# Thirteen dots at the boundaries and in the index scores, their low parts by transfer; wide block pairs in both feed-forwards

## The chip, the cores and the metric

The kernel runs on one core of a Trainium2 chip. The metric is the device time of one execution in microseconds (us). Before the change the median of three timed executions is 1220.28 us (1219.72 to 1220.76).

The core has five engines that each work through their own list of instructions in order: PE multiplies matrices (PEld is its weight load), DVE and ACT work element by element, POOL and SP here issue most of the transfers between HBM and the on-chip memory. An instruction that waits for another engine holds up all that stands behind it on its own engine.

## What is computed

Two layers of a decoder trunk on 512 positions of width 1024, all float32. Layer 0 has stick-breaking attention, layer 1 the indexer-selected sparse attention (DSA). Each mixer and each feed-forward is preceded by a norm whose shift, scale and gate come from the vector c.

```python
def conv_ffn(h, w_up, conv_w, conv_b, w_down):
    S = h.shape[1]
    u = h @ w_up
    up = jnp.pad(u, ((0, 0), (CONV_W - 1, 0), (0, 0)))
    y = conv_b
    for j in range(CONV_W):
        y = y + up[:, j:j + S] * conv_w[j]
    gate, val = jnp.split(y, 2, axis=-1)
    return (jax.nn.silu(gate) * val) @ w_down
```

The shift, scale and gate of a layer are c times a 1024 x 6144 matrix plus a bias: 48 columns of 128 numbers for each layer, six groups of eight. In the DSA layer the projection of h gives queries (16 heads of 128), one latent of 128, index queries (8 heads of 64), index keys and head weights; the index scores, a sum over the eight heads of relu(qi . ki) times a weight, choose the keys.

## The kernel before, in words

**Float32 by parts.** A weight chunk is 128 x 1024 float32 (512 KB). SP loads it into a place of the ring `raw` (`chunk_raw`), ACT copies it to the rounded high part `whi` (`split_hi`, a copy shown at L613), and then the low part `wlo` = raw - whi is made in one of two ways. `split_lo` (L622) is one DVE subtraction. `split_sum` (its ACT line is L630, its transfer L631) is two steps: ACT writes minus the *raw* chunk, rounded, into `wlo`, and POOL then issues a transfer that reads the chunk from HBM a second time and adds it into `wlo`. Inside the planned feed-forwards the same pair of steps stands at L1491 (ACT) and L1495 (POOL). `mm3` (L663 to L665) multiplies three times: high by high, then **low weight** by high, then high by low; so the low part is wanted by the second matmul of a product.

**The adaLN dots.** One of the 48 columns is one DVE instruction over a loaded 128 x 1024 chunk and c (`ada_dot`, L691). Layer 1 has 48 of them, numbered (1, group, column). Before the change they are done in feed-forward 0 (37, groups 0 to 4 but for three), in the DSA layer (three, `LATE_DOTS`) and in feed-forward 1 (eight, group 5).

**Boundaries.** `boundary` joins two stages: it ends a projection (eight row blocks m, tiles pt_l), adds them to x, and while the norm of the new x is worked out PE already runs the next projection's first four row blocks (tiles pt_first): two from the scaled but unnormed x (`xs`), two from the normed `hh`. The chunks of those four are split in the same loop: the third one's high part in step m = 6, its low part in m = 7, the fourth one's right after the loop. Boundary 0 leads to feed-forward 0, boundary 1 (which has a `begin`) to the DSA layer and its index scores, boundary 2 to feed-forward 1. Places of `raw` come free when a chunk has been split; then SP loads the next.

**Index scores.** For each of the eight index heads h PE makes three score products z (tiles of 256, 384 and 512 columns, two banks), ACT takes each one's relu (L1990), DVE adds it up; the matmuls of the next projections (pt_lat, then pt_q of the chunks dq) stand between them. After heads 0, 1, 4 and 6 a chunk dq is split with `prefetch`: low part of the chunk before, high part of the next one, low part at once.

**Feed-forwards.** 22 blocks j of 128 columns for gate and val each. Blocks 0 to 6 are plain. Blocks from 7 on are computed as pairs of 256 columns with seven products instead of eight (a1, d1, a2, e, d2, c1, c2), twelve matmuls each: four chunks of the weight, times high and low of the activation (eight matmuls of 256 columns) and low weight times high (four). For a block in `MERGED` the high and low activation stand side by side, so that the eight become four matmuls of 512 columns (L1594); the second half lands in the other half of the bank, and DVE adds it to the result after each evacuation (`side`, six additions of 128 x 256 a block). `down` multiplies the finished blocks by the down matrix, its low part by DVE, or by transfer (`DOWN_DMA`); the result is added to x by DVE (L785), or scaled by ACT (L1694) and added by a transfer (L1697, `X_DMA`). In `ACT_DMA` the low part of a block's activation is made by transfer.

`ffn_plan` orders all of it: each step is a job with an engine, a duration and what it waits for. `Plan.order` runs PE's jobs in the order written, and lets every other engine take, whenever it is free, the ready job with the earliest due time. That order is then written out as the engines' instruction lists. `LEADS`, the free times at the start and `DOT_SPAN` are the numbers it works with.

Of the kernel before, what the change touches and what calls it, by code (L numbers as in the profile page):

```python
# [21 lines left out]
KT = D // P  # L22
# [40 lines left out]
DOWNS_7 = [[(7, 1), (8, 2), (9, 2), (10, 1), (11, 2), (12, 2), (13, 1), (14, 1), (15, 1), (16, 2), (17, 1), (18, 2), (19, 2),  # L63
# [10 lines left out]
DOT_SPAN = [(10, 320), (0, 150)]  # L74
PLAIN_DMA = [[(4, 0), (4, 1), (5, 0), (5, 1), (6, 0)], [(4, 0), (4, 1), (5, 1), (6, 0), (6, 1)]]
DOWN_DMA = [[6, 13, 22], [0, 3, 4, 6, 8, 12, 13, 15, 16, 17, 20, 22]]
LEADS = [{'plain': 33.5, 'r': 20.0, 'sum': 16.0, 'down': 13.5, 'T': 40.0, 'last': 36.5, 'bias': 12.5},
         {'plain': 78.5, 'r': 3.5, 'sum': 0.5, 'down': 6.5, 'T': 8.5, 'last': 11.0, 'bias': 15.5}]
DOT_GROUPS = [[(1, 0), (1, 1), (1, 2), (1, 3), (1, 4)], [(1, 5)]]
LATE_DOTS = [(1, 4, 5), (1, 4, 6), (1, 4, 7)]  # L80
FFN_BIAS = [(1, 12), (1, 17)]
MERGED = [[], [10, 11, 12, 13, 14, 15, 16, 17, 18, 19, 20, 21]]
X_DMA = [[0, 1, 2, 3, 5, 7, 8, 10, 14, 18, 19, 21, 23], []]
ACT_DMA = [[3, 4, 18], []]
XT = 2

# [15 lines left out]
class Plan:  # L102
# [44 lines left out]
    def order(self):  # L147
# [23 lines left out]
        out = []  # L171

        def ready(j):
            if any(a.end is None for a in j.after) or any(a.start is None for a in j.behind):
                return None
            t = max((a.end + (a.lag if a.engine != j.engine or a.lag > 1 else 0.0) for a in j.after), default=0.0)
            return max([t] + [a.start for a in j.behind])

        while len(out) < len(self.jobs):
# [4 lines left out]
            while moved:  # L184
                moved = False
                for e, q in queues.items():
                    if not q or free[e] > now:
                        continue
                    can = [(r, i) for i, j in enumerate(q[:1] if e == "PE" else q) for r in [ready(j)] if r is not None and r <= now]
                    if not can:  # L190
                        continue
                    j = q.pop(min(can)[1] if e == "DMA" else can[0][1])
# [18 lines left out]
def ffn_plan(l):  # L211
# [3 lines left out]
    p = Plan(dict(DVE=13.0, ACT=12.0, SP=-5.0, DMA=-5.0, POOL=-5.0))  # L215
# [11 lines left out]
    for n, t in enumerate((-9, -9, 0.0, 1.5, 6.3, 7.5)):  # L227
# [315 lines left out]
def kernel_body(ctx, tc, xT, wst, cst, smalls, crow, ccol, relb, outT):  # L543
# [152 lines left out]

    def ada_steps(n):
# [104 lines left out]
    def boundary(n, last, O, l, gate, nxt, first, place, begin=None, after_scale=None):  # L802
# [9 lines left out]
        goals = {0: last[2], 1: last[3], 2: first[0], 4: first[1], 6: first[2]}  # L812

# [12 lines left out]
        for m in range(KT):  # L826
# [19 lines left out]
            split_lo()  # L846
# [12 lines left out]
        split_lo()  # L859
# [24 lines left out]
        for k in range(KT + 1):  # L884
# [544 lines left out]
    def ffn_layer(l, first, man):  # L1429
        with ExitStack() as st:  # L1430
# [23 lines left out]
            split_lo()  # L1454
# [304 lines left out]
    def dsa_layer(l, first, man):  # L1759
        with ExitStack() as st:  # L1760
# [118 lines left out]
            with ExitStack() as si:  # L1879
# [100 lines left out]
                for h in range(IDX_HEADS):  # L1980
# [12 lines left out]
                    if h in (0, 1, 4, 6):  # L1993
                        prefetch(pos["i"])
# [64 lines left out]
            with ExitStack() as sa:  # L2059
# [62 lines left out]
                def late_dots(n):  # L2122
                    for _ in range(n):
                        (_, g, f), raw = raw_dots.pop(0)
                        ada_dot(mod[l][:, g * KT + f:g * KT + f + 1], raw)
                        if f == KT - 1:
                            ada_sum(l, g)
# [335 lines left out]
```

## Time and profile before

| | |
|---|---|
| median of three executions | 1220.28 us |
| the profiled execution | 1219.72 us |
| its span in the trace (1.8 us lie around it) | 1217.9 us |
| granted TensorE clock | 1.00 |
| stick-breaking layer | 0 to 238 us |
| boundary 0 | 238 to 280.5 |
| feed-forward 0, plain blocks and block pairs | 280.5 to 335, 335 to 586 |
| boundary 1 | 586 to 626 |
| index scores | 634 to 659 |
| choice of keys, projections, DSA heads | to 846 |
| boundary 2 | 846 to 891 |
| feed-forward 1, of it block pairs | 891 to 1193, 946 to 1193 |
| end | to 1217.9 |

The rows of the timeline shown below read: start in us, duration in us, engine, line, operation, output <- inputs, shape, and in brackets the engine's idle time ahead of it with what ended it. SPq and POOL rows of DMA_DIRECT2D are issues of transfers, not the transfers themselves. A matmul's duration overlaps the next one's; the distance of two starts is what it costs.

### The profile page before, as it was taken

What the parts mean: (1) busy time and instruction counts of PE and PEld (TensorE: products, weight loads), DVE (VectorE), ACT (ScalarE), POOL (GpSimd) and SP (SyncE); (2) the same over time, 40 slices, a digit from 0 to 9 for tenths busy, and PEclk for the clock granted to TensorE, in tenths of its full rate; (3) what the DMA queues carried; (4) which work ended last, traced back from release to release, by engine and by line L of the source; (5) the groups of instructions that cost most, each with busy time, mean ns of one, the idle gap of its engine ahead of it and who ended that gap; (6) DMA issues with size and microseconds to landing.
All of it is one profiled execution on the core that took longest, in us unless ns stands there. A gap on an engine that the chain in (4) does not pass through costs nothing.

```text
span 1217.9 us, 18663 instructions
## 1 busy us (share of the span) xinstructions
PE 1211.9 (100%) x6768; PEld 1023.7 (84%) x6768; DVE 1040.5 (85%) x1786; ACT 785.7 (65%) x1348; POOL 218.3 (18%) x240
## 2 busy tenths in 40 slices
PE   9999999999999999999999999999999999999998
PEld 6888787788899999999888778777888998888887
DVE  5899889999989889887788996668998989889883
ACT  5587786467677667666556357774676576676650
POOL 0000000000112111111001357774001112111100
PEclk9999999999999999999999999999999999999999
DMA  9678685624999989797622311144459787777651
GB/s 376 234 194 216 194 225 196 198 73 138 245 235 247 257 233 248 211 248 191 201 70 71 103 52 53 52 124 139 136 155 216 213 186 161 181 180 174 159 132 69
DMA packets 66651, 212.77 MB, mean 175 GB/s; under 512 B 7808, under 2 KB 8576, under 8 KB 66560
## 3 DMA queue, kind: packets, MB, share of 16 engines
q1 hardware_dynamic: 50400, 166.88, 41.3%
q0 software_dynamic: 16160, 44.71, 21.0%
q8 instruction: 53, 0.87, 0.3%
q14 instruction: 38, 0.31, 0.1%
HBM read 205.25 MB, written 2.11 MB: 170 GB/s over the span
## 4 chain that ended last, share of the span: by engine, by line
PE 94%; DVE 4%; ACT 1%; issue 1%; DVEq 0%; ACTq 0%
PE pt_d L1686 16%; PE pt_a L1598 10%; PE pt_u L1567 6%; PE pt_d L1598 5%; PE pt_a L1594 4%; PE pt_u L1571 3%; PE pt_b L1598 3%; PE pt_q L663 2%; PE pt_q L665 2%; PE pt_q L664 2%; PE pt_qk L663 2%; PE pt_qk L664 2%; PE pt_qk L665 2%; PE pt_l L663 2%; PE pt_l L665 2%; PE pt_l L664 2%
## 5 line engine op out<-in xcount | busy, mean ns | idle before, releaser
L1686 PE MATMUL pt_d<-actlo,dnhi 128*128 128x512 f32 x288 | 112.7, 391 | 0.0
L1686 PE MATMUL pt_d<-acthi,dnhi 128*128 128x512 f32 x288 | 112.6, 391 | 0.0
L1495 POOL DMA_DIRECT2D wlo<-wst x40 | 34.7, 867 | 363.7 <-ACT wlo L1491 296.1
L1483 ACT ACTIVATE whi<-raw 128x1024 fp32r<-128x1024 f32 x72 | 75.7, 1053 | 27.4 <-PE pt_a L1598 17.5
L613 ACT ACTIVATE whi<-raw 128x1024 fp32r<-128x1024 f32 x80 | 84.0, 1052 | 1.2 <-PE pt_o L665 0.9
L1567 PE MATMUL pt_u<-hh,whi 128*128 128x512 f32 x320 | 75.8, 389 | 0.0
L1686 PE MATMUL pt_d<-acthi,dnlo 128*128 128x512 f32 x288 | 73.5, 390 | 0.0
L1567 PEld LDWEIGHTS pt_u<-hh,whi 128*128 128x128 f32 x320 | 60.1, 188 | 12.5
L622 DVE TENSOR_TENSOR wlo<-raw,whi 128x1024 fp32r<-128x1024 f32 x51 | 62.0, 1219 | 3.1 <-ACT whi L613 2.8
L1686 PEld LDWEIGHTS pt_d<-actlo,dnhi 128*128 128x128 f32 x288 | 54.2, 188 | 10.2
L1686 PEld LDWEIGHTS pt_d<-acthi,dnhi 128*128 128x128 f32 x288 | 54.2, 188 | 10.0
L1686 PEld LDWEIGHTS pt_d<-acthi,dnlo 128*128 128x128 f32 x288 | 53.1, 188 | 10.3
L1598 PE MATMUL pt_a<-hh,whi 128*128 128x256 f32 x432 | 60.4, 283 | 0.0
L1598 PEld LDWEIGHTS pt_a<-hh,whi 128*128 128x128 f32 x432 | 57.5, 191 | 2.3
L622 POOL TENSOR_TENSOR wlo<-raw,whi 128x1024 fp32r<-128x1024 f32 x18 | 44.0, 2452 | 84.9 <-PE pt_q L664 46.1
L691 DVE SCALAR_TENSOR_TENSOR ada<-ada,cond 128x1024 f32<-128x1024 f32 x45 | 54.8, 1218 | 3.9 <-DMA ada<-wst 3.8
L1598 PE MATMUL pt_a<-hh,wlo 128*128 128x256 f32 x360 | 57.6, 282 | 0.0
L1306 DVE TENSOR_TENSOR_SCAN mz<-mz,diag 128x128 f32<-128x128 f32 (+1 forms) x64 | 52.4, 818 | 3.4 <-ACT mz L1301 3.2
L1874 DVE CUSTOM_DVE_ANT_0 L<-z,L,cols 128x128 f32<-128x128 f32 (+3 forms) x60 | 32.5, 547 | 26.2 <-PE tr L2170 19.9
L1598 PEld LDWEIGHTS pt_a<-hh,wlo 128*128 128x128 f32 x360 | 51.8, 191 | 2.9
L691 DVE SCALAR_TENSOR_TENSOR raw<-raw,cond 128x1024 f32<-128x1024 f32 x42 | 52.6, 1279 | 1.4 <-ACT cond L1127 1.3
L1506 POOL DMA_DIRECT2D whi<-wst x30 | 25.9, 864 | 152.6 <-ACT whi L1503 60.9
(391 smaller groups left out, 3750.2 us busy)
## 6 DMA issues: line engine op xcount, KB each, us to landing
raw<-wst SPq DMA_DIRECT2D x211, 512.0 KB, 4.9
wlo<-wst POOLq DMA_DIRECT2D x51, 512.0 KB, 7.5
ada<-wst SPq DMA_DIRECT2D x49, 512.0 KB, 5.3
raw<-wst SPq DMA_DIRECT2D x48, 384.0 KB, 4.6
whi<-wst POOLq DMA_DIRECT2D x30, 256.0 KB, 5.3
dnlo<-wst POOLq DMA_DIRECT2D x15, 384.0 KB, 7.3
th<-relb SPq DMA_DIRECT2D x16, 256.0 KB, 3.3
x<-xt POOLq DMA_DIRECT2D x13, 256.0 KB, 6.8
```

Source lines behind the costliest of these rows:

```text
L613: act.activation(hi[:, :n], raw[:, :n], AF.Copy)
L622: engine.tensor_sub(lo[:, :w], raw[:, :w], hi[:, :w].bitcast(F32))
L663: pe.matmul(out, lhsT=whi, rhs=ahi, start=start, stop=False)
L664: pe.matmul(out, lhsT=wlo, rhs=ahi, start=False, stop=False)
L665: pe.matmul(out, lhsT=whi, rhs=alo, start=False, stop=stop)
L691: dve.scalar_tensor_tensor(raw, raw, 1.0, cond, op0=OP.mult, op1=OP.mult, accum_out=dst)
L1306: dve.tensor_tensor_scan(rev, rev, diag[:, S - ns:][:, ::-1], 0.0, OP.mult, OP.max)
L1483: act.activation(W[j, i][0], R[j, i], AF.Copy)
L1567: pe.matmul(pt[j, i], lhsT=W[j, i][0][:, k * P:(k + 1) * P], rhs=hs[k][n], start=k + n == 0, stop=False)
L1594: pe.matmul(pt[j, bank, "both"], lhsT=w[:, c0 + k * P:c0 + (k + 1) * P], rhs=a[2], start=new and k == 0, stop=False, skip_group_check=True)
L1598: pe.matmul(out, lhsT=w[:, c0 + k * P:c0 + (k + 1) * P], rhs=a[n], start=new and k + n == 0, stop=part == 1 and k == 3 and what in ("a2", ...
L1686: pe.matmul(pt["dn", i], lhsT=dn[i][part][:, k * P:(k + 1) * P], rhs=A[j0 + k][n], start=part + k + n == 0, stop=part == 1 and k == j1 - j ...
```

## The change

13 of layer 1's dots leave the feed-forwards (feed-forward 0 has 27 in place of 37, feed-forward 1 five in place of eight). Three are done at each boundary, with chunks loaded into `raw` (`edge_dot`), four in the index scores after heads 0, 1, 4 and 6. At the same places DVE's subtraction goes and the low part is made by `split_sum`: three chunks at each boundary, four in the index scores, and at boundaries 0 and 2 four more each, in the loop of the norm and at the start of the feed-forward: 21 in all, while one plain chunk of feed-forward 1 goes back to DVE. In the feed-forwards nine more blocks are merged (eight in feed-forward 0, one net in feed-forward 1, 54 more side additions), and transfers take over eight more additions to x and five more low parts of activations; which down chunks go by transfer is changed (three to six, and twelve to nine). The planner's start values follow. `Plan.order` is written in another way (queues by readiness in place of a search), with the same rule.

```diff
-DOWNS_7 = [[(7, 1), (8, 2), (9, 2), (10, 1), (11, 2), (12, 2), (13, 1), (14, 1), (15, 1), (16, 2), (17, 1), (18, 2), (19, 2),
+DOWNS_7 = [[(7, 1), (8, 1), (9, 2), (10, 2), (11, 2), (12, 2), (13, 1), (14, 1), (15, 2), (16, 1), (17, 1), (18, 2), (19, 2),
...
-DOT_SPAN = [(10, 320), (0, 150)]
-PLAIN_DMA = [[(4, 0), (4, 1), (5, 0), (5, 1), (6, 0)], [(4, 0), (4, 1), (5, 1), (6, 0), (6, 1)]]
-DOWN_DMA = [[6, 13, 22], [0, 3, 4, 6, 8, 12, 13, 15, 16, 17, 20, 22]]
-LEADS = [{'plain': 33.5, 'r': 20.0, 'sum': 16.0, 'down': 13.5, 'T': 40.0, 'last': 36.5, 'bias': 12.5},
-         {'plain': 78.5, 'r': 3.5, 'sum': 0.5, 'down': 6.5, 'T': 8.5, 'last': 11.0, 'bias': 15.5}]
-DOT_GROUPS = [[(1, 0), (1, 1), (1, 2), (1, 3), (1, 4)], [(1, 5)]]
-LATE_DOTS = [(1, 4, 5), (1, 4, 6), (1, 4, 7)]
-FFN_BIAS = [(1, 12), (1, 17)]
-MERGED = [[], [10, 11, 12, 13, 14, 15, 16, 17, 18, 19, 20, 21]]
-X_DMA = [[0, 1, 2, 3, 5, 7, 8, 10, 14, 18, 19, 21, 23], []]
-ACT_DMA = [[3, 4, 18], []]
+DOT_SPAN = [(10, 320), (0, 160)]
+PLAIN_DMA = [[(4, 0), (4, 1), (5, 0), (5, 1), (6, 1)], [(4, 1), (5, 1), (6, 0), (6, 1)]]
+DOWN_DMA = [[4, 6, 13, 18, 19, 21], [0, 3, 4, 7, 8, 13, 15, 16, 20]]
+LEADS = [{'plain': 35.0, 'r': 18.5, 'sum': 14.5, 'down': 12.0, 'T': 43.0, 'last': 12.5, 'bias': 23.0},
+         {'plain': 84.5, 'r': 3.5, 'sum': 0.5, 'down': 0.5, 'T': 11.5, 'last': 15.5, 'bias': 18.5}]
+FFN_BIAS = [(1, 11), (1, 13)]
+MERGED = [[10, 11, 12, 14, 16, 19, 20, 21], [7, 8, 10, 11, 12, 14, 15, 16, 17, 18, 19, 20, 21]]
+X_DMA = [[3, 4, 5, 7, 8, 10, 12, 13, 14, 19, 20, 23], [0, 2, 6, 8, 12, 16, 19, 20, 21]]
+ACT_DMA = [[2, 4, 5, 12], [2, 4, 8, 15]]
 XT = 2
+DOTS = [(1, g, f) for g in range(6) for f in range(8)]
+EDGE_DOTS = [DOTS[:3], DOTS[30:33], DOTS[40:43]]
+KEY_DOTS = DOTS[33:37]
+LATE_DOTS = DOTS[37:40]
+FFN_DOTS = [DOTS[3:30], DOTS[43:]]
...
-
-        def ready(j):
-            if any(a.end is None for a in j.after) or any(a.start is None for a in j.behind):
-                return None
+        out, wait, later, now_ready = [], {}, {e: [] for e in queues}, {e: [] for e in queues}
+        rank = {id(j): i for q in queues.values() for i, j in enumerate(q)}
+        turn = {e: 0 for e in queues}
+        needs = {id(j): [] for j in self.jobs}
+
+        def release(j):
             t = max((a.end + (a.lag if a.engine != j.engine or a.lag > 1 else 0.0) for a in j.after), default=0.0)
-            return max([t] + [a.start for a in j.behind])
+            j.ready = max([t] + [a.start for a in j.behind])
+            heapq.heappush(later[j.engine], (j.ready, rank[id(j)], j))
...
 def ffn_dots(l):
-    jobs = [g + (f,) for g in DOT_GROUPS[l] for f in range(KT)]
+    jobs = list(FFN_DOTS[l])
     if l == 0:
-        jobs = jobs[:len(jobs) - len(LATE_DOTS)]
         for n, at in FFN_BIAS:
             jobs.insert(at, ("bias", n, "row" if ("bias", n, "col") in jobs else "col"))
     return jobs
...
-    p = Plan(dict(DVE=13.0, ACT=12.0, SP=-5.0, DMA=-5.0, POOL=-5.0))
+    p = Plan(dict(DVE=10.5, ACT=12.5, SP=-5.0, DMA=-5.0, POOL=-5.0))
...
-    for n, t in enumerate((-9, -9, 0.0, 1.5, 6.3, 7.5)):
+    for n, t in enumerate((-9, -9, -5.0, -3.0, 4.7, 5.7)):
...
+    def one_dot(d, raw):
+        l, g, f = d
+        ada_dot(mod[l][:, g * KT + f:g * KT + f + 1], raw)
+        if f == KT - 1:
+            ada_sum(l, g)
...
+        edge = list(EDGE_DOTS[n])
+
+        def edge_dot():
+            d = edge.pop(0)
+            one_dot(d, chunk_raw(("ada",) + d))
...
-            split_lo()
+            if m in (3, KT - 1):
+                split_sum()
+                edge_dot()
+            else:
+                split_lo()
             if m in goals:
                 while pos["i"] <= order.index(goals[m]):
                     split_hi()
...
         split_hi()
-        split_lo()
+        split_sum()
+        edge_dot()
...
-            if k in (4, 6):
+            if k in ((4, 6) if begin else (1, 3)):
                 split_hi()
+            if k in (2, 4) and not begin:
+                split_sum()
             if k == 6:
                 rescale(0)
         if begin:
             begin(vs[0])
-        split_lo(n=1)
+            split_lo(n=1)
         rescale(1)
...
             pts, vs = first
-            split_lo()
             es = [evac_scale(0, i, vs[i]) for i in range(2)]
             split_hi()
             split_hi(ahead=0)
             ys = [evac_conv(e) for e in es]
-            split_lo()
             es = [evac_scale(1, i, pts[2 + i]) for i in range(2)]
+            split_sum()
+            split_sum()
             warm(AF.Silu)
             ys += [evac_conv(e) for e in es]
...
                     if h in (0, 1, 4, 6):
-                        prefetch(pos["i"])
+                        split_lo()
+                        split_hi()
+                        split_sum()
+                        d = KEY_DOTS[(0, 1, 4, 6).index(h)]
+                        one_dot(d, chunk_raw(("ada",) + d))
                     elif h == 2:
```

The counts over the program: PE has 504 fewer matmuls of 256 columns and 252 more of 512; DVE 20 fewer low subtractions, eight fewer additions to x, five fewer low parts of activations, 54 more side additions; ACT 20 more copies of a chunk with minus sign, eight more scaled results, five more copies of activations; POOL issues 33 more transfers, SP as many as before (352).

**ACT at the end of boundary 0's loop.** The rows run from the splitting of the third chunk (raw_2548, raw_2552 after) to the norm's logarithm `ln`. Before:

```order
L613 ACTIVATE whi_2599<-raw_2548 128x1024
L723 ACTIVATE sqt_2615<-x3_92 128x512
L836 ACTIVATE xkz70_2617<-x3_92,sm_76 128x512
L731 ACTIVATE sqhi_2622<-sqa_2469 128x512
L613 ACTIVATE whi_2636<-raw_2597 128x1024
L757 ACTIVATE ln_2664<-pt_norm_2661,ecols_80 128x512
```

After:

```order
L642 ACTIVATE whi_2603<-raw_2552 128x1024
L758 ACTIVATE sqt_2619<-x3_92 128x512
L876 ACTIVATE xkz70_2621<-x3_92,sm_76 128x512
L766 ACTIVATE sqhi_2626<-sqa_2469 128x512
L659 ACTIVATE wlo_2631<-raw_2552 128x1024
L642 ACTIVATE whi_2644<-raw_2601 128x1024
L659 ACTIVATE wlo_2646<-raw_2601 128x1024
L792 ACTIVATE ln_2676<-pt_norm_2673,ecols_80 128x512
```

Two ACT copies to a `wlo` stand new between the sum of squares (sqhi) and `ln`: the third chunk's, and behind the fourth chunk's high part (whi_2644) the fourth's. Behind each of them POOL issues its transfer. PE's order there is unchanged: the third chunk's product starts with the first normed column (hh_2430), the fourth's stands three matmuls behind. Boundaries 1 and 2 have the same four rows.

**ACT in the index scores, head 0 to head 2.** rl is the relu of a score product z. Before:

```order
L1990 ACTIVATE rl_6568<-z_6562 128x512
L613 ACTIVATE whi_6573<-raw_6439 128x1024
L1990 ACTIVATE rl_6583<-z_6577 128x256
L1990 ACTIVATE rl_6592<-z_6586 128x384
L1990 ACTIVATE rl_6601<-z_6595 128x512
L613 ACTIVATE whi_6606<-raw_6571 128x1024
L1990 ACTIVATE rl_6616<-z_6610 128x256
L1990 ACTIVATE rl_6625<-z_6619 128x384
L1990 ACTIVATE rl_6635<-z_6628 128x512
```

After:

```order
L2037 ACTIVATE rl_6400<-z_6394 128x512
L642 ACTIVATE whi_6405<-raw_6271 128x1024
L659 ACTIVATE wlo_6407<-raw_6271 128x1024
L2037 ACTIVATE rl_6419<-z_6413 128x256
L2037 ACTIVATE rl_6428<-z_6422 128x384
L2037 ACTIVATE rl_6437<-z_6431 128x512
L642 ACTIVATE whi_6442<-raw_6403 128x1024
L659 ACTIVATE wlo_6444<-raw_6403 128x1024
L2037 ACTIVATE rl_6456<-z_6450 128x256
L2037 ACTIVATE rl_6465<-z_6459 128x384
```

The negative copy of the dq chunk (wlo_6407, wlo_6444) stands behind its high part and ahead of the next head's three relus.

**PE and DVE in feed-forward 0.** Six of the seven products of block 10, the first merged one, on PE (a1, d1, a2, e, d2, c1). Before:

```order
L1598 MATMUL pt_a<-hh,whi 128x256 x8
L1598 MATMUL pt_a<-hh,wlo 128x256 x4
L1598 MATMUL pt_d<-tt,whi 128x256 x8
L1598 MATMUL pt_d<-tt,wlo 128x256 x4
L1598 MATMUL pt_b<-hh,whi 128x256 x12
L1598 MATMUL pt_a<-tt,whi 128x256 x8
L1598 MATMUL pt_a<-tt,wlo 128x256 x4
L1598 MATMUL pt_d<-tt,whi 128x256 x8
L1598 MATMUL pt_d<-tt,wlo 128x256 x4
L1598 MATMUL pt_a<-hh,whi 128x256 x8
L1598 MATMUL pt_a<-hh,wlo 128x256 x4
```

After:

```order
L1641 MATMUL pt_a<-hh,whi 128x512 x4
L1645 MATMUL pt_a<-hh,wlo 128x256 x4
L1641 MATMUL pt_d<-tt,whi 128x512 x4
L1645 MATMUL pt_d<-tt,wlo 128x256 x4
L1641 MATMUL pt_b<-hh,whi 128x512 x4
L1645 MATMUL pt_b<-hh,whi 128x256 x4
L1641 MATMUL pt_a<-tt,whi 128x512 x4
L1645 MATMUL pt_a<-tt,wlo 128x256 x4
L1641 MATMUL pt_d<-tt,whi 128x512 x4
L1645 MATMUL pt_d<-tt,wlo 128x256 x4
L1641 MATMUL pt_a<-hh,whi 128x512 x4
L1645 MATMUL pt_a<-hh,wlo 128x256 x4
```

Each product's eight matmuls of 256 columns have become four of 512. On DVE, in the next merged block, from its second evacuation:

```order
L1681 TENSOR_TENSOR vx<-vx,pt_d 128x256
L1665 TENSOR_TENSOR gate<-gate,pt_b 128x256
L1681 TENSOR_TENSOR gate<-gate,pt_b 128x256
L1700 TENSOR_TENSOR actlo<-y_3844,acthi 128x512
L1693 TENSOR_TENSOR y_3970<-y_4035,y_3970 128x512
L1681 TENSOR_TENSOR vx<-vx,pt_a 128x256
L1717 TENSOR_TENSOR dnlo<-raw,dnhi 128x768
L1675 TENSOR_TENSOR val<-vx,pt_d 128x256
```

The side additions (L1681) of vx, gate and vx again are new rows; product c1 (pt_a from tt before it is e) waits for the second of vx, for which DVE must have done the rows ahead of it.

More of the change, by code (lines that the diff above doesn't have):

```diff
@@ L170, in order @@
         times = sorted(set(free.values()))
-        out = []
-        def ready(j):
-            if any(a.end is None for a in j.after) or any(a.start is None for a in j.behind):
-                return None
-            t = max((a.end + (a.lag if a.engine != j.engine or a.lag > 1 else 0.0) for a in j.after), default=0.0)
-            return max([t] + [a.start for a in j.behind])
+        out, wait, later, now_ready = [], {}, {e: [] for e in queues}, {e: [] for e in queues}
[3 more added lines that the diff above has]
+        def release(j):
+            t = max((a.end + (a.lag if a.engine != j.engine or a.lag > 1 else 0.0) for a in j.after), default=0.0)
+            j.ready = max([t] + [a.start for a in j.behind])
+            heapq.heappush(later[j.engine], (j.ready, rank[id(j)], j))
+        for j in self.jobs:
+            j.ready = None
+            wait[id(j)] = len(j.after) + len(j.behind)
+            for a in j.after + j.behind:
+                needs[id(a)].append(j)
+        for j in self.jobs:
+            if not wait[id(j)]:
+                release(j)
         while len(out) < len(self.jobs):
@@ L186, in order @@
                 for e, q in queues.items():
-                    if not q or free[e] > now:
+                    if free[e] > now:
                         continue
[L189 to L192, printed above, removed]
+                    if e == "PE":
+                        if turn[e] >= len(q) or q[turn[e]].ready is None or q[turn[e]].ready > now:
+                            continue
+                        j = q[turn[e]]
+                        turn[e] += 1
+                    elif e == "DMA":
+                        if not later[e] or later[e][0][0] > now:
+                            continue
+                        j = heapq.heappop(later[e])[2]
+                    else:
+                        while later[e] and later[e][0][0] <= now:
+                            r, i, j = heapq.heappop(later[e])
+                            heapq.heappush(now_ready[e], (i, j))
+                        if not now_ready[e]:
+                            continue
+                        j = heapq.heappop(now_ready[e])[1]
                     j.start, j.end = now - 1e-9, now - 1e-9 + j.us
@@ L198, in order @@
                     moved = True
+                    for n in needs[id(j)]:
+                        wait[id(n)] -= 1
+                        if not wait[id(n)]:
+                            release(n)
         return [j for j in out if j.fn]
 def ffn_dots(l):
-    jobs = [g + (f,) for g in DOT_GROUPS[l] for f in range(KT)]
+    jobs = list(FFN_DOTS[l])
     if l == 0:
-        jobs = jobs[:len(jobs) - len(LATE_DOTS)]
         for n, at in FFN_BIAS:
@@ L845, in boundary @@
                 squares_lo()
[L846 removed]
+            if m in (3, KT - 1):
+                split_sum()
+                edge_dot()
+            else:
+                split_lo()
             if m in goals:
@@ L2123, in late_dots @@
                     for _ in range(n):
[L2124 to L2127, printed above, removed]
+                        one_dot(*raw_dots.pop(0))
                 def masked_bias(h, j):
```

## The prediction

> **What bounds the kernel now.** I read the busy shares first, then the chain of work that ended last, then PE's waits past the start (60 us to the end).
>
> ```profile
> PE 1211.9 (100%) x6768; PEld 1023.7 (84%) x6768; DVE 1040.5 (85%) x1786; ACT 785.7 (65%) x1348; POOL 218.3 (18%) x240
> ```
>
> ```profile
> PE 94%; DVE 4%; ACT 1%; issue 1%; DVEq 0%; ACTq 0%
> ```
>
> ```profile
> PE pt_o L663 <- DVE x L785: 0.3, 1, 0.3
> ```
>
> PE is never idle: 94% of the chain is PE's own matmuls, and behind the start it waited for another engine once, 0.3 us. So the time falls only by what PE no longer has to do, and rises by every wait that PE meets and did not meet before. What DVE is spared is worth nothing by itself. That makes two questions: what do the wider pairs take off PE, and does anything that PE wants now come later?
>
> **The wide pairs.** PE's rows of the down product's first matmul, at the end of one block and of the next, in feed-forward 0 (eight matmuls of 256) and in feed-forward 1 (four of 512), each with one down in between:
>
> ```profile
> 343.52 0.40 PE L1686 MATMUL pt_d<-acthi,dnhi 128*128 128x512 f32 x1
> ...
> 357.70 0.40 PE L1686 MATMUL pt_d<-acthi,dnhi 128*128 128x512 f32 x1
> ```
>
> ```profile
> 1003.30 0.40 PE L1686 MATMUL pt_d<-acthi,dnhi 128*128 128x512 f32 x1
> ...
> 1017.22 0.40 PE L1686 MATMUL pt_d<-acthi,dnhi 128*128 128x512 f32 x1
> ```
>
> A block takes 357.70 - 343.52 = 14.18 us the old way and 1017.22 - 1003.30 = 13.92 the wide way. Nine more wide blocks give 9 x 0.26 = **-2.3 us**.
>
> Their price is on DVE, six side additions a block; the rows are a group of these in feed-forward 1's pairs, the group of the dots on a raw chunk, and the busy times of the two stages of pairs:
>
> ```profile
> L1634 DVE TENSOR_TENSOR vx<-vx,pt_a 128x256 f32<-128x256 f32 x12 | 5.0, 420 | 2.4 <-ACT vx L1611 2.2
> ```
>
> ```profile
> L691 DVE SCALAR_TENSOR_TENSOR raw<-raw,cond 128x1024 f32<-128x1024 f32 x42 | 52.6, 1279 | 1.4 <-ACT cond L1127 1.3
> ```
>
> ```profile
> 335.00:586.00 251.00, 251.00 (x1700) 233.40 (x1699) 217.66 (x322) 164.78 (x252) 38.47 (x45) 1.00 0.88 236
> 946.00:1193.00 247.00, 247.00 (x1360) 214.84 (x1359) 219.43 (x353) 161.90 (x247) 33.81 (x39) 1.00 0.70 169
> ```
>
> In the last two rows DVE is the entry behind PE and PEld: 217.66 of 251 us and 219.43 of 247. 48 additions of 0.42 are 20 us in feed-forward 0, and the ten dots that leave give back about 13 (10 x 1.28); DVE there stays below 93%, and in feed-forward 1, where transfers take nine additions to x and four low parts, it gets lighter. The shares leave room. The one tight place is c1: it waits for the side addition of e's copy, and in feed-forward 0 only d2, about 1.4 us of PE (a seventh of 14.18 less the down's 18 matmuls of 0.23), lies between, against a copy of 0.4, an addition of 0.42 and the matmul's own end of 0.4, with whatever DVE has just begun in front. The rows of DVE's new order have actlo and a product, 0.7 each, ahead of it in block 11, which PE's a2, e and d2 just cover. In feed-forward 1 the same chain runs with a down in between and PE does not wait. I take **+0.5** for all eight; bounds 0 and 8 (a whole instruction of about 1.2 less 0.2 of slack, eight times).
>
> **The low parts by transfer.** Now one DVE instruction is replaced by an ACT copy, an issue on POOL and a transfer. How long is that?
>
> ```profile
> DMA to landing us min/median/max: 5.5/7.5/11.6
> ```
>
> ```profile
> 294.21 0.87 POOL L1495 DMA_DIRECT2D wlo<-wst  x1 [119.78 <-ACT wlo L1491]
> ```
>
> ```profile
> 295.71 0.33 SPq L1713 DMA_DIRECT2D ada<-wst  x1
> 296.14 0.68 SPq L582 DMA_DIRECT2D raw<-wst  x1
> ```
>
> ```profile
> 296.77 0.87 POOL L1495 DMA_DIRECT2D wlo<-wst  x1 [1.69 <-ACT wlo L1491]
> ```
>
> ```profile
> DMA to landing us min/median/max: 9.2/9.2/9.2
> ```
>
> The first row is over all transfers into wlo, from issue to landing: 5.5 us at the shortest. The other rows show one that found POOL's queue empty and the next one, 2.56 us later, with two plain loads issued between them; the last row is the second one's own landing, 9.2 us, that is 296.77 + 9.2 - 294.21 = 11.8 us after the *first* one's issue. I use that as the rule for a pair. By the share of the queue,
>
> ```profile
> q0 software_dynamic: 16160, 44.71, 21.0%
> ```
>
> 512 KB (0.524 MB) of POOL's queue hold all 16 engines for 0.21 x 1217.9 x 0.524 / 44.71 = 3.0 us, so a pair with no load between cannot end before 5.5 + 3.0 = 8.5 us behind the first issue.
>
> [...]
>
> **The ends of the boundaries.** ACT's last high part, and PE's matmuls that want the third and the fourth chunk's low part, at boundaries 0, 1 and 2:
>
> ```profile
> 261.10 1.04 ACT L613 ACTIVATE whi<-raw 128x1024 fp32r<-128x1024 f32 x1
> ...
> 269.84 0.39 PE L664 MATMUL pt_first<-hh,wlo 128*128 128x512 f32 x1
> ...
> 270.52 0.39 PE L664 MATMUL pt_first<-hh,wlo 128*128 128x512 f32 x1
> ```
>
> ```profile
> 609.54 1.04 ACT L613 ACTIVATE whi<-raw 128x1024 fp32r<-128x1024 f32 x1
> ...
> 618.52 0.39 PE L664 MATMUL pt_first<-hh,wlo 128*128 128x512 f32 x1
> ```
>
> ```profile
> 871.91 1.04 ACT L613 ACTIVATE whi<-raw 128x1024 fp32r<-128x1024 f32 x1
> ...
> 880.89 0.39 PE L664 MATMUL pt_first<-hh,wlo 128*128 128x512 f32 x1
> ```
>
> In the place of that one copy stand three (negative, high, negative), started 0.95 us apart (637.87 and 638.82 below). So at boundary 0 the third chunk's transfer is issued at 261.10 + 1.05 = 262.15 and the fourth's at 264.05, two loads going out between as raw's places come free. The third has 269.84 - 262.15 = 7.7 us, about the median. The fourth is issued 6.5 us before PE wants it, behind the third. By the pair rule it lands at 262.15 + 11.8 = 273.95: PE waits 3.4. At boundary 1: issue 610.59, landing 622.4, wanted 618.52: 3.9. At boundary 2: 872.96, 884.75, 880.89: 3.9. Together **+11.2**. What stands behind the waiting matmul is all of PE, which nothing shortens later. Bounds: with no load between (8.5 us) the waits are 0.1, 0.6 and 0.6, 1.3 in all; with the longest landing seen, 11.6 from the fourth's own issue, 5.1, 5.6 and 5.6, 16.3 in all. I take the pair because its queue looks the same. A wait for an earlier low part holds PE but not ACT, so it takes as much from these waits and adds nothing. The dots themselves (1.28 on DVE in place of a subtraction of much the same length) and `ln`, which slips 0.4 to 0.8 behind the copies, reach PE only through the norm, behind the same wait. The four low parts at the feed-forwards' starts are wanted after a product's 16 high matmuls; their cover is those matmuls, and I price them at nothing.
>
> **The index scores.**
>
> ```profile
> 637.87 1.05 ACT L613 ACTIVATE whi<-raw 128x1024 fp32r<-128x1024 f32 x1
> 638.82 0.38 ACT L1990 ACTIVATE rl<-z 128x256 f32<-128x256 f32 x1
> ...
> 650.66 1.05 ACT L613 ACTIVATE whi<-raw 128x1024 fp32r<-128x1024 f32 x1
> ```
>
> ```profile
> 639.85 0.39 PE L1986 MATMUL z<-kd,qs 128*128 128x512 f32 x1
> ...
> 643.67 0.39 PE L664 MATMUL pt_q<-hh,wlo 128*128 128x512 f32 x1
> ...
> 660.28 0.39 PE L664 MATMUL pt_q<-hh,wlo 128*128 128x512 f32 x1
> ```
>
> After head 0 the negative copy ends at 638.82 + 1.05 = 639.87, and PE wants the low part at 643.67, 3.8 us later. With a landing of 5.5 to 7.5, PE waits 1.7 to 3.7; the loads of a dot's and of the next dq's chunk are released at the same moment, so I take 6.5: **+2.7**. Head 4's (copy at 650.66, issue 652.7, wanted 660.28) has 7.6, the median; nothing for it or for the two others. The copy also holds the next relu: 638.82 + 0.38 + 0.95 = 640.15, where the third z at 639.85 wants its bank, 0.3; after heads 0 and 1 that is inside the wait, after 4 and 6 it is **+0.6**.
>
> **Sum.** 1219.7 (the profiled execution) - 2.3 + 0.5 + 11.2 + 2.7 + 0.6 = 1232.4. The median of the runs is 0.6 above the profiled one; I say **1232.4**, which lies between.
>
> **Rivals.**
> 1. *Gain only.* The low parts come in time everywhere, because the queues are emptier at the boundaries than where the pair was seen. 1219.7 - 2.3 + 0.6 = 1218.0. For it: PE needs only 6.5 and 3.8 us that are a little under the shortest seen for one transfer and far under for a pair; against it: those shortest, 5.5 and 8.5. To fall on this side a pair must land within 8.3 us and a lone transfer within 3.8. Chance 0.10, and a little over half of it stays within 0.2%.
> 2. *Early landing.* The loads do not come between and a transfer takes 5.5 to 7.5. With 8.5 for the pair: 1219.7 - 2.3 + 1.3 + 1.7 + 1.1 = 1221.5; with 7.5 from its own issue the fourth chunk costs 1.0 + 1.5 + 1.5 and dq0's 3.7: 1226.2. Chance 0.24.
> 3. *c1 is late in feed-forward 0.* DVE begins something long just before each side addition; up to +8 on top of the forecast: 1236 to 1240. The share of DVE (87%) speaks for it, the planned order against. Chance 0.10.
> 4. *The change does not take hold*: DVE's freed time brings nothing and the low parts are taken from elsewhere; about 1220. The order shows both edits, so 0.04.
>
> The forecast, 1228 to 1236, has 0.52. The range 1220 to 1238 leaves out most of the first rival and the end of the third. A measurement of this kernel tells 0.2% (2.4 us) from no change: faster 0.05, within 0.2% 0.16 (rivals 1 and 4, and the low end of 2), slower 0.79.
>
> **What would show it.** PE waits for DMA wlo at L693 once near each boundary's third to fourth product (3 to 4 us) and once at the first pt_q of the index scores (about 2.7); the transfers there land 9 to 10 us (the fourth chunk's) and 6 to 7 us (dq0's) after their issue; wide blocks of feed-forward 0 repeat after 13.9 us, and no wait for the vx side addition exceeds some tenths. The prediction is wrong if PE's waits stay below 2 us in all, or if they come up in the feed-forwards.

## The result, and the profile after

The changed kernel takes 1236.58 us (median of four runs, 1236.33 to 1237.81); the ratio to before is 1.0136, with a 95% interval of 1.0118 to 1.0153. It is slower by about 16.3 us. The forecast was 1232.4 in a range of 1220 to 1238, slower with 0.79.

The page of the kernel after, PE's share and the chain that ended last:

```profile
PE 1216.8 (98%) x6516; PEld 1012.0 (82%) x6516; DVE 1035.5 (84%) x1816; ACT 812.2 (66%) x1381; POOL 247.0 (20%) x273
```

```profile
PE 85%; DMA 5%; issue 4%; DVE 4%; ACT 2%; POOL 1%; SPq 0%; DVEq 0%; POOLq 0%; ACTq 0%
```

PE holds 85% of the chain in place of 94%; transfers, which were not in it at all, hold 5%. The waits of PE past the start, in the same kernel:

```profile
PE pt_first L693 <- DMA wlo<-wst: 8.4, 7, 2.2
PE pt_q L693 <- DMA wlo<-wst: 4.0, 2, 3.7
PE z L2033 <- ACT rl L2037: 0.8, 4, 0.2
PE pt_o L692 <- DVE x L820: 0.3, 1, 0.3
```

Only the last row stood there before. L693 is the low weight's matmul of `mm3`, and it waits nine times for the second transfer of a chunk: that is the forecast's mechanism. Stage by stage, from the starts of the first matmuls of pt_l, pt_u, pt_lat and of the end in both timelines:

| stage | before | after | difference |
|---|---|---|---|
| up to boundary 0 | 235.8 | 235.5 | -0.3 |
| boundary 0 | 44.7 | 49.3 | +4.7 |
| feed-forward 0 | 304.0 | 301.8 | -2.2 |
| boundary 1, to the index scores | 50.5 | 56.0 | +5.5 |
| index scores to boundary 2 | 211.9 | 220.3 | +8.4 |
| boundary 2 | 44.3 | 47.1 | +2.8 |
| feed-forward 1 | 300.8 | 300.5 | -0.3 |
| end | 26.0 | 25.5 | -0.5 |

The sum is 18.1 us, the difference of the two spans (1236.0 and 1217.9). The feed-forwards gave 2.5 us, and the other places took 21.

The landing of the transfers: two issues on POOL at the end of boundary 0 and one in the index scores, each with its own time to landing.

```profile
262.12 0.86 POOL L660 DMA_DIRECT2D wlo<-wst  x1 [11.02 <-ACT wlo L659]
```

```profile
DMA to landing us min/median/max: 8.5/8.5/8.5
```

```profile
264.02 0.86 POOL L660 DMA_DIRECT2D wlo<-wst  x1 [1.03 <-PE pt_norm L774]
```

```profile
DMA to landing us min/median/max: 9.1/9.1/9.1
```

```profile
647.81 0.86 POOL L660 DMA_DIRECT2D wlo<-wst  x1 [24.14 <-ACT rl L2037]
```

```profile
DMA to landing us min/median/max: 8.2/8.2/8.2
```

The pair lands 264.02 + 9.1 - 262.12 = 11.0 us behind its first issue (11.7 and 10.6 at boundaries 1 and 2, worked out in the same way); the rule had 11.8. The lone one of the index scores takes 8.2, where 6.5 was taken. Beside each issue stand loads of SP, which wait for the same copy on ACT and go out some 0.26 us ahead of POOL's issue. That these loads lengthen the landing is likely, but not shown: no run has the transfers without them. In e5 (below), where the next load and the next transfer follow the third chunk's issue 3.5 and 3.8 us later in place of 0.7 and 1.9, it landed after 8.3, 6.5 and 6.5 us at the three boundaries, where the change has 8.5, 7.9 and 8.1.

What no step of the forecast had is in PE's rows behind such a wait, here in the after kernel at boundary 0:

```profile
273.15 0.50 PE L693 MATMUL pt_first<-hh,wlo 128*128 128x512 f32 x1 [1.56 <-DMA wlo<-wst]
273.49 0.39 PE L694 MATMUL pt_first<-hh,whi 128*128 128x512 f32 x1
273.72 0.59 PE L692 MATMUL pt_first<-hh,whi 128*128 128x512 f32 x1
274.11 0.63 PE L693 MATMUL pt_first<-hh,wlo 128*128 128x512 f32 x1
274.53 0.63 PE L694 MATMUL pt_first<-hh,whi 128*128 128x512 f32 x1
```

From 273.72 on the starts are 0.39 to 0.43 us apart, where those of the same matmul were 0.23 apart in the kernel before. The busy times by stretches of 4 us (the last entries are the granted clock, the share of the DMA engines and GB/s) show the same:

```profile
270.00:274.00 4.00, 2.04 (x8) 1.25 (x7) 3.85 (x6) 4.00 (x6) 0.86 (x1) 0.97 1.01 284
274.00:278.00 4.00, 4.00 (x12) 3.09 (x12) 3.71 (x7) 3.17 (x6) 0.86 (x1) 0.60 1.03 314
...
622.00:626.00 4.00, 1.78 (x7) 1.17 (x6) 4.00 (x7) 2.70 (x5) 1.67 (x5) 0.92 0.85 282
626.00:630.00 4.00, 4.00 (x13) 3.11 (x13) 3.62 (x7) 3.63 (x6) 0.00 (x0) 0.66 0.02 4
...
654.00:658.00 4.00, 1.91 (x6) 1.62 (x7) 1.28 (x2) 0.22 (x1) 0.00 (x0) 0.76 1.03 267
```

The clock was 1.00 all through the kernel before. Behind three of the waits it falls to 0.50 for 3.41 us, and what is missing to 1.00 in these five stretches is 4 x (0.03 + 0.40 + 0.08 + 0.34 + 0.24) = 4.4 us; the third fall reaches some way past 658. Matmul by matmul, against the same matmuls before, the three falls cost 1.6, 1.6 and 1.4 us: 4.6 in all.

### The profile page after: what moved, and what is told of

The parts are those of the page before. It is cut to its first block, busy times and chain, and to the rows that moved or that the text cites. A ratio compares the mean times of both kernels' runs of the same rounds, so it can differ in the third digit from the quotient of the medians.

```text
span 1236.0 us, 18294 instructions
## 1 busy us (share of the span) xinstructions
PE 1216.8 (98%) x6516; PEld 1012.0 (82%) x6516; DVE 1035.5 (84%) x1816; ACT 812.2 (66%) x1381; POOL 247.0 (20%) x273
## 4 chain that ended last, share of the span: by engine, by line
PE 85%; DMA 5%; issue 4%; DVE 4%; ACT 2%; POOL 1%; SPq 0%; DVEq 0%; POOLq 0%; ACTq 0%
PE pt_d L1733 16%; PE pt_a L1645 7%; PE pt_a L1641 6%; PE pt_u L1614 6%; DMA wlo<-wst 5%; PE pt_d L1645 4%; PE pt_d L1641 3%; PE pt_u L1618 3%; PE pt_qk L692 2%; PE pt_qk L693 2%; PE pt_qk L694 2%; PE pt_q L693 2%; PE pt_q L694 2%; PE pt_q L692 2%; PE pt_b L1645 2%
## 5 line engine op out<-in xcount | busy, mean ns | idle before, releaser
L660 POOL DMA_DIRECT2D wlo<-wst x32 | 27.7, 866 | 341.9 <-DVE raw L720 103.5
L720 DVE SCALAR_TENSOR_TENSOR raw<-raw,cond 128x1024 f32<-128x1024 f32 x55 | 68.8, 1272 | 1.4 <-ACT cond L1174 1.3
L1641 PE MATMUL pt_a<-hh,whi 128*128 128x512 f32 x252 | 67.7, 390 | 0.0
L1542 POOL DMA_DIRECT2D wlo<-wst x39 | 33.8, 867 | 169.1 <-ACT wlo L1538 115.6
L693 PE MATMUL pt_q<-hh,wlo 128*128 128x512 f32 x128 | 50.8, 397 | 4.0 <-DMA wlo<-wst 4.0
L1641 PEld LDWEIGHTS pt_a<-hh,whi 128*128 128x128 f32 x252 | 46.2, 188 | 8.8
```

The source lines that it names most:

```text
L693: pe.matmul(out, lhsT=wlo, rhs=ahi, start=False, stop=False)
L720: dve.scalar_tensor_tensor(raw, raw, 1.0, cond, op0=OP.mult, op1=OP.mult, accum_out=dst)
L1641: pe.matmul(pt[j, bank, "both"], lhsT=w[:, c0 + k * P:c0 + (k + 1) * P], rhs=a[2], start=new and k == 0, stop=False, skip_group_check=True)
```

## The experiments

Two theories stood against each other. *Late parts*: everything lost is PE's waits for low parts that come by transfer, with the slow matmuls behind them, and the wide blocks pay 2.5 us. *Crowding*: the dots themselves, and what the change adds on DVE and ACT, do not fit at these places, however the low parts are made.

**e1, e2, e3: the low parts by DVE again, the dots in place.** In all places (e1), in the index scores alone (e2), at the boundaries and the feed-forwards' starts alone (e3).

```diff
-                        split_sum()
+                        split_lo()
                         d = KEY_DOTS[(0, 1, 4, 6).index(h)]
...
             if m in (3, KT - 1):
-                split_sum()
+                split_lo()
                 edge_dot()
...
         split_hi()
-        split_sum()
+        split_lo()
         edge_dot()
...
             if k in (2, 4) and not begin:
-                split_sum()
+                split_lo()
...
-            split_sum()
-            split_sum()
+            split_lo()
```

> All 21 low parts of the boundaries, the feed-forwards' starts and the index scores are made by DVE again; the 13 dots stay where the change put them, and the feed-forwards are those of the change. Theory (PE's waits for low parts that come by transfer, and the half-speed matmuls behind those waits, are the whole loss): PE's 12.4 us of waits for DMA wlo, some 4.6 us of slow matmuls and 0.8 us of waits for relus go, about 1219 us. Rival (the dots themselves crowd DVE at the boundaries): DVE now has the subtraction and the dot, about 1.2 us more at each of nine places with DVE at 85 to 95% there, PE waits for DVE in place of the transfer, 1225 us or more.

> Only the four low parts of the index scores are made by DVE again. Theory: the index scores' loss of about 8 us (3.9 and 0.5 for transfers, 1.6 for relus, about 1.2 of slow matmuls, and what is left) goes, about 1228.5 us; the boundaries' waits stay. Rival (the dots crowd DVE in the index scores): at most half of it goes, 1232 us or more.

> Only the 17 low parts of the boundaries and of the feed-forwards' starts are made by DVE again, the index scores keep the transfers. Theory: 2.8 + 3.9 + 2.8 us of waits and about 3.3 of slow matmuls go, about 1224 us. Rival (crowded DVE): 1229 us or more.

Measured, against 1219.78 before: e1 1232.96 (ratio 1.0108, 1.0092 to 1.0123), e2 1227.63 (1.0064, 1.0049 to 1.0079), e3 1240.74 (1.0173, 1.0158 to 1.0188). In the index scores the theory of the late parts holds: with the low parts by DVE 9 us go. In the profiled executions 7.8 of them lie in that stage (220.3 to 212.5, where it was 211.9 before), so the dots cost 0.7 there. The boundaries 0 and 1 of e2, which it does not edit, are 2.1 and 1.7 us shorter as well: in its profiled execution the same waits left the clock at 1.00. At the boundaries the theory fails: e3 is *slower* than the change. PE's waits in e1:

```profile
PE pt_first L692 <- ACT hh L806: 6.3, 3, 2.6
PE pt_first L694 <- DVE hh L810: 3.4, 6, 0.8
```

The waits for transfers are gone and waits for the normed column hh have come in their place. The DVE rows of e1 at boundary 0 (first the two dots, then the norm's first step), and behind them the norm's first step in the kernel before:

```profile
263.16 1.22 DVE L720 SCALAR_TENSOR_TENSOR raw<-raw,cond 128x1024 f32<-128x1024 f32 x1
...
266.10 1.22 DVE L720 SCALAR_TENSOR_TENSOR raw<-raw,cond 128x1024 f32<-128x1024 f32 x1
...
267.25 0.69 DVE L797 TENSOR_TENSOR nt<-ln 128x512 f32<-128x512 f32 x1
```

```profile
264.77 0.69 DVE L762 TENSOR_TENSOR nt<-ln 128x512 f32<-128x512 f32 x1
```

The norm starts 267.25 - 264.77 = 2.5 us later, about the two dots of 1.22: DVE is the path there as soon as it has subtraction and dot.

**e10: the boundary dots left out.** e1, with a 128 x 1 memset in the place of each boundary dot.

```diff
-            d = edge.pop(0)
-            one_dot(d, chunk_raw(("ada",) + d))
+            l_, g, f = edge.pop(0)
+            dve.memset(mod[1][:, g * KT + f:g * KT + f + 1], 0.0)
+            if f == KT - 1:
+                ada_sum(1, g)
```

> e1 (all low parts by DVE again, dots in place) with the nine dots at the boundaries and their loads left out, a 128 x 1 memset in the place of each; nine columns of layer 1's modulation are not computed, so the output isn't the reference's. Theory (in e1 and e3 PE waits for hh because the dots hold DVE in front of the norm: the subtraction and the dot do not both fit): e1's 10 us of waits for hh and the slow matmuls behind them go, 1218 to 1220 us. Rival (what holds the norm is that low parts were moved into the norm's loop, steps k = 2 and 4, or the ACT order there): at least a third of the waits stays, 1223 us or more.

Measured: 1222.33 us (ratio 1.0019, 1.0010 to 1.0028), between the two expectations. The waits by ACT, 6.3 us, are gone altogether; these are the dots'. What is left of the other row:

```profile
PE pt_first L694 <- DVE hh L810: 2.8, 6, 0.8
```

So the rival had a part: these 2.8 us come without any dot, at boundaries 0 and 2, where the low parts stand inside the norm's loop (k = 2 and 4), 1.22 us on DVE in front of the next hh. The two at boundary 0:

```profile
270.64 1.22 DVE L651 TENSOR_TENSOR wlo<-raw,whi 128x1024 fp32r<-128x1024 f32 x1
...
274.43 1.22 DVE L651 TENSOR_TENSOR wlo<-raw,whi 128x1024 fp32r<-128x1024 f32 x1
```

**e4: PE kept busy while it waits.**

```diff
+FILLERS = [[2, 0, 2, 7], [6, 0, 0, 10], [7, 0, 0, 4]]
+FILL_KEY = 16
...
             for i in ids:
+                for _ in range(FILLERS[n][i] if k == 0 else 0):
+                    pe.matmul(pts[i], lhsT=cs[i][0][:, w], rhs=src[k][0], start=True, stop=False, skip_group_check=True)
                 mm3(pts[i], cs[i][0][:, w], cs[i][1][:, w], src[k][0], src[k][1], k == 0, k == KT - 1)
```

> The changed kernel with matmuls that only fill PE's time while it waits: 2, 7, 6, 10, 7 and 4 repeats of a product's first matmul ahead of the boundaries' late products and 16 ahead of the first dq product, each overwritten by the next. Nothing else is changed; the low parts land no earlier. Theory (the matmuls at twice the spacing behind the waits come from PE having been idle): they go, about 4.6 us less, 1232 us. Rival (they come from something else at those places, for example the transfers or ACT and DVE working on the same memory): no change, 1236 to 1238 us.

Measured: 1235.05 us, 1.5 less than the change; in the profiled executions 3.2 less (spans 1232.8 and 1236.0). The stretch at the same place:

```profile
274.00:278.00 4.00, 4.00 (x19) 3.31 (x18) 3.71 (x6) 3.17 (x5) 0.86 (x1) 1.00 0.99 336
```

19 matmuls in place of 12, at 1.00. In all four executions of e4 the granted clock is 1.000 over the whole run, where the four of the change have 0.996 to 0.997. So the slow matmuls do come from PE having waited. The time fell by less than the 4.6 expected: boundaries 0 and 1 became 2.2 and 1.7 us shorter, but the index scores did not, since the first dq transfer, issued at 644.35, landed 9.6 us later in place of 8.2 and took back what the clock gave.

**e5: the transfers issued earlier.** e2, with the negative copies of the first and third chunk right behind their high parts.

```diff
-            if m in (3, KT - 1):
-                split_sum()
-                edge_dot()
-            else:
-                split_lo()
+            split_lo()
+            if m in (3, KT - 1):
+                edge_dot()
             if m in goals:
                 while pos["i"] <= order.index(goals[m]):
                     split_hi()
+                if m in (2, 6):
+                    split_sum()
```

> On top of e2 (low parts of the index scores by DVE): at the boundaries the negative copy of the first and of the third chunk stands right behind its high part, in step 2 and in step 6, in place of steps 3 and 7; the dots stay. The transfers of the first and third chunk are issued some 2 to 3 us earlier, the fourth's 0.95 us earlier. Theory (PE waits at the boundaries because the transfers are issued too late, and for nothing else): e2's 8.7 us of waits for DMA wlo fall to 0 to 2 us, 1219 to 1221 us. Rival (DVE's and ACT's new work at the boundaries holds the norm as soon as the transfers are out of the way, as the low parts by DVE did in e3): waits for hh by ACT or DVE come up, 1223 us or more.

Measured: 1224.86 us (ratio 1.0040, 1.0026 to 1.0054), 2.8 below e2 and 4 to 6 above the expectation.

```profile
PE pt_first L693 <- DMA wlo<-wst: 4.1, 3, 1.6
```

Of e2's waits the earlier chunks' are gone; three, one at each boundary, stay. They are the fourth chunk's, whose high part e5 leaves where it was and whose transfer again had some 6.6 us; it landed 8.3 us after its issue at boundary 0 (265.66 to 273.96). The theory was right about what waits, and had the fourth chunk's transfer too cheap: with the third's issue 3.8 us ahead of it in place of 1.9 it still took 8.3, 8.6 and 7.7 us at the three boundaries (9.1, 9.8 and 8.7 in the change).

**e6, e7: where the dots have to be.** e6 is e2 with the boundaries as before and their nine dots back in the feed-forwards; e7 is the kernel before with nothing but the change's list of wide blocks.

```diff
-EDGE_DOTS = [DOTS[:3], DOTS[30:33], DOTS[40:43]]
...
-FFN_DOTS = [DOTS[3:30], DOTS[43:]]
+FFN_DOTS = [DOTS[:33], DOTS[40:]]
...
```

```diff
-MERGED = [[], [10, 11, 12, 13, 14, 15, 16, 17, 18, 19, 20, 21]]
+MERGED = [[10, 11, 12, 14, 16, 19, 20, 21], [7, 8, 10, 11, 12, 14, 15, 16, 17, 18, 19, 20, 21]]
```

> The boundaries and the feed-forwards' starts as before the change; their nine dots are back in the feed-forwards (33 and eight dots in place of 27 and five); the wide blocks, the tables of transfers and the dots in the index scores (with low parts by DVE, as in e2) stay. Theory (the wide blocks bring 2.5 us, index dots with low parts by DVE cost about 1, and DVE, 90% busy in feed-forward 0's pairs, takes six more dots): 1218 to 1219.5 us. Rival (the dots had to leave the feed-forwards for the wide blocks' side additions): PE waits for DVE in feed-forward 0, 1221 us or more.

> The kernel before with the change's list of wide blocks alone: eight more in feed-forward 0 and one net in feed-forward 1, all dots and all other tables as before. Theory (DVE limits): in feed-forward 0's pairs DVE has 217.7 + 20 us of work in 249, 95%, side additions come late and PE waits for c1 in some blocks, 1220 to 1226 us. Rival (DVE has room and only the sum over the stage matters): 1217.5 us.

Measured: e6 1227.16 us (ratio 1.0059, 1.0044 to 1.0074), e7 1221.83 (1.0014, 1.0005 to 1.0024). PE's longest waits, of e6 and then of e7:

```profile
PE pt_d L1719 <- ACT xt L1727: 6.0, 1, 6.0
```

```profile
PE pt_a L1594 <- DVE vx L1634: 2.8, 2, 1.5
```

e6's boundaries cost what they did before (44.7, 50.5 and 44.3 us), and with 33 dots in feed-forward 0 no c1 waits; its one long wait, in feed-forward 1, is for a scaled result on its way to x, which waits for the gate, that is for the last of eight dots where the change has five. The expectation had overlooked that chain. e7 shows the wait for c1 that the prediction had as its third rival: with all dots in feed-forward 0 and the old tables, the side addition of vx is late in two blocks, 1.5 and 1.3 us, and eats what the wide blocks give: feed-forward 0 is 1.6 us longer than before, where the change's is 2.2 shorter.

**e8, e9, e11, e12: in search of a version that pays.** Here the planner's tables were chosen anew. e8: four dots in the index scores, boundaries as before, 7 and 13 wide blocks. e9: no dot moved, 6 and 13. e11 and e12: the same two with feed-forward 1 as before and five and three wide blocks, with tables under which the dots end within feed-forward 0. The core of e11 against the kernel before (the dots' lists and the other tables of feed-forward 0 are left out):

```diff
-MERGED = [[], [10, 11, 12, 13, 14, 15, 16, 17, 18, 19, 20, 21]]
-X_DMA = [[0, 1, 2, 3, 5, 7, 8, 10, 14, 18, 19, 21, 23], []]
-ACT_DMA = [[3, 4, 18], []]
+MERGED = [[12, 14, 15, 19, 20], [10, 11, 12, 13, 14, 15, 16, 17, 18, 19, 20, 21]]
+X_DMA = [[0, 7, 10, 11, 12, 13, 15, 18, 21, 23], []]
+ACT_DMA = [[2, 3, 4, 7, 8, 12, 15], []]
+KEY_DOTS = DOTS[33:37]
...
-                        prefetch(pos["i"])
+                        split_lo()
+                        split_hi()
+                        split_lo()
+                        d = KEY_DOTS[(0, 1, 4, 6).index(h)]
+                        one_dot(d, chunk_raw(("ada",) + d))
```

> e6 (boundaries as before, four dots in the index scores with low parts by DVE, the rest in the feed-forwards) with the planner's start values of before and with the feed-forwards' tables chosen anew, so that gate dots of feed-forward 1 come early enough for its additions to x by transfer: 7 and 13 wide blocks. Theory (e6's 6.1 us wait and the slow matmuls behind it come from those additions standing ready before the gate): it goes, 1219.9 - 7 x 0.27 - 0.27 - 0.5 for PE's small waits that leave + 0.8 for the index scores = about 1218 us. Rival (feed-forward 0 has no room for 33 dots and wide blocks): 1220 us or more.

> No dot is moved: boundaries and index scores as before the change, 37 and eight dots in the feed-forwards; 6 and 13 wide blocks, with more additions to x and low parts of activations by transfer and the planner's tables chosen anew (e7 had the wide blocks with the old tables). Theory (the wide blocks need DVE time where they stand, not the dots' going; other tables find it): 1219.9 - 6 x 0.27 - 0.27 - 0.3 = about 1217.7 us. Rival (37 dots leave no room, as in e7): 1220 us or more.

> As e8, with feed-forward 1 exactly as before the change (eight dots, 12 wide blocks), and feed-forward 0 with 33 dots and five wide blocks, tables chosen so that the dots end with the stage (in e8 and e9 they ran on past it and held the next boundary). Theory: 1220.0 - 5 x 0.27 - 0.3 + 0.8 for the index scores = about 1219.2 us, not to be told from before. Rival (the dots still run late, or the index scores cost more): 1221 us or more.

> No dot is moved, feed-forward 1, boundaries and index scores as before the change; feed-forward 0 with all 37 dots and three wide blocks (12, 20, 21), tables chosen so that the dots end with the stage. Theory: 1220.0 - 3 x 0.27 = 1219.2 us, not to be told from before. Rival (DVE has no room at all beside 37 dots): 1221 us or more.

Measured: e8 1226.13 us and e9 1243.46, both misses. Feed-forward 0 was as short as hoped (302.1 and 302.3 us from pt_u to pt_l, where it was 304.0), but the dots had been pushed past its end, into boundary 1. PE's longest wait there in e9:

```profile
PE pt_l L689 <- ACT whi L639: 22.2, 1, 22.2
```

The chunks that the boundary splits stood behind the late dots' loads in SP's list, and each of those loads waited for the place of the dot before it. SP's issues there in e9:

```profile
578.36 30.13 SPq L1744 DMA_DIRECT2D ada<-wst  x7
608.54 9.20 SPq L608 DMA_DIRECT2D raw<-wst  x7
```

e11, whose dots end with the stage, took 1218.97 us (ratio 0.9991, 0.9982 to 0.9999) and e12 1219.74 (0.9997, 0.9988 to 1.0005); 1219.2 was expected of both. e11 is faster than the kernel before by about a thousandth of the time, with an interval that only just leaves out no change, and it is the best of four versions; e12 can't be told from before.

## Why the prediction was right

The direction, the places and the mechanism were right: PE waits for low parts that land late. The time is in part luck. It lies just above the forecast's own band of 1228 to 1236, in the band of the third rival, whose wait did not come. The terms of the sum came to 12.9 us in place of 12.7 (-2.5 for the blocks, 9.6 at the boundaries, 5.8 in the index scores), because terms that were too large and one that was too small cancelled; what the time lies above the forecast is for the most part the clock, which no term had.

- *PE is the bound, only its work and its waits count*: so it was. DVE's busy time fell from 1040.5 to 1035.5 us, and nothing came of that.
- *The wide blocks*, -2.3: the feed-forwards became 2.2 and 0.3 us shorter. The +0.5 for c1 did not come; PE has no wait for vx in the change. e7 shows that the third rival's mechanism exists: with all dots there and the old tables, c1 waits 2.8 us. The new tables avoid it even with 33 dots there (e6); how much of that the dots' going bought is not separated. The side additions are seven a block, not the six that the description and the forecast count (84 before, 147 after): 56 x 0.42 = 23.5 us in feed-forward 0, with which the forecast's own sum of DVE, 217.66 + 23.5 - 13, is 228 of 251 us. DVE in the pairs of feed-forward 0 after:

```profile
335.00:586.00 251.00, 251.00 (x1486) 223.27 (x1485) 225.13 (x357) 167.35 (x256) 40.40 (x47) 1.00 0.88 232
```

  225.13 of 251 us, 90%, where the forecast allowed 93%.
- *The ends of the boundaries*, +11.2: PE's waits by the gaps between the starts were 0.5 + 0.6 + 1.7 at boundary 0, 1.6 + 2.4 at boundary 1 and 1.7 + 1.1 at boundary 2, 9.6 in all, 1.6 less than the forecast. The pair rule held within about a tenth (11.0, 11.7 and 10.6 us for 11.8), and the waits for the earlier chunks did add nothing of their own: at boundary 1 1.6 + 2.4 is the 3.9 that was forecast for the one wait.
- *The index scores*, +2.7 and +0.6: it was 8.4. Two of PE's rows there:

```profile
651.42 0.50 PE L2033 MATMUL z<-kd,qs 128*128 128x512 f32 x1 [0.20 <-ACT rl L2037]
...
656.09 0.79 PE L693 MATMUL pt_q<-hh,wlo 128*128 128x512 f32 x1 [3.70 <-DMA wlo<-wst]
```

  By the gaps between the starts the first dq's wait was 3.9, since the transfer took 8.2 us and not 6.5; the relus' waits were 0.35 after each of the four heads, 1.4; the fourth dq waited 0.5 where the forecast had nothing. That is 5.8 of waits, and 1.4 of slow matmuls comes on top. Direction and place were right, and the terms were too small by 2.5 us of waits.
- *The clock*: the term that was missing. 4.6 us of the 18.1 lie in matmuls at a granted clock of 0.50 behind three waits, which the row of clocks of the kernel before (1.00) could not show. Without it the time would be about 1232.
- *The gain-only rival* is refuted: pairs landed in 10.6 to 11.7 us where it needed 8.3, and the lone transfer in 8.2 where it needed 3.8. (The forecast's words for it hold a slip: PE's 6.5 us are above the shortest landing of 5.5, not under it.) No transfer into wlo landed in less than 5.3 us in the changed kernel.
- Some 1.2 us between the index scores and boundary 2 lie in differences below 0.3 us each and are not assigned.
- What the forecast did not see, because it never had to: had the low parts come in time, the dots would have stood in the norm's way next (e1, e3, e10). In the change each dot takes the time of the subtraction that it displaces (1.22 us each; the norm's first step starts at 264.56 us at boundary 0, where it was 264.77), so only the transfer's lateness shows. That is also why the low parts at a boundary can't go back to DVE by themselves with profit (e3), while e2's step in the index scores can be undone. The other half at a boundary, the dots out and the transfers kept, was not run.

## What to carry to other kernels

Before a low part, or any operand, goes from an engine to a transfer, subtract the moment of issue from the moment when the in-order consumer wants it, and compare that with landings of transfers that had others in front; here 6.5 us stood against 8.7 to 9.8 at the boundaries. An edit that swaps one piece of work for another on a busy engine has two costs to ask about, the new one's delay and what the freed time was spent on. A stage made shorter on paper by letting its low-priority work run late pays at the next stage's start, in e9 with a wait of PE of 22.2 us.

## What the runs showed of the hardware that was not expected

PE's granted clock fell to 0.50 for 3.41 us behind waits that were short: in the change behind 0.6 and 1.7 us in one go at boundary 0, behind 2.4 at boundary 1 and behind 3.9 in the index scores. It did not do so each time: in the same kernel the 1.6 of boundary 1 and the 1.7 of boundary 2, and in e2 waits of 1.8, 2.2 and 2.3, left it at 1.00, and in e1 2.6 at boundary 1 brought it down and 2.8 at boundary 2 did not.

The clock records of the change's trace show where the falls lie. They begin at 273.75, 625.33 and 656.05 us and last 3.41 us each, and their starts lie on one grid: 625.33 - 273.75 is 103 x 3.413, 656.05 - 625.33 is 9 x 3.413. On that grid PE was idle for 1.85, 2.22 and 3.41 us in the stretches just ahead of the three falls, and for at most 1.54 us in any other stretch between 60 and 1200 us. Here are the change's fall at boundary 1 and, on the grid of e1's own fall, e1's wait at boundary 2 (behind the length of the stretch stands PE's busy time; the third entry from the end is the clock):

```profile
621.92:625.33 3.41, 1.19 (x5) 0.67 (x4) 3.41 (x6) 2.11 (x4) 1.75 (x6) 1.00 1.00 330
625.33:628.74 3.41, 3.41 (x9) 2.64 (x8) 3.41 (x7) 3.04 (x5) 0.00 (x0) 0.50 0.04 11
```

```profile
886.28:889.69 3.41, 2.10 (x10) 1.41 (x8) 2.88 (x6) 0.00 (x0) 0.00 (x0) 1.00 0.38 130
889.69:893.10 3.41, 2.06 (x8) 1.35 (x9) 3.28 (x6) 2.89 (x4) 0.00 (x0) 1.00 0.91 338
893.10:896.51 3.41, 2.65 (x12) 1.93 (x11) 3.41 (x5) 1.70 (x4) 0.00 (x0) 1.00 0.62 193
```

With 2.2 us idle in one stretch the clock came down; with 1.3 and 1.35 in two neighbours it did not, though the wait across them was longer. Counted over all the runs here, from 60 us to the end of feed-forward 1, the clock fell from 1.00 eleven times, each time behind a stretch with 1.76 (in e5) to 3.41 us idle, and never behind one with 1.62 or less.
